# Modulation weights of the retention stage loaded from GpSimd's DMA queue instead of SyncE's

## The chip, the cores and the metric

The kernel runs on one core of a Trainium2 chip. The metric is the device time of one execution in microseconds (us). The engines are named as in the profile: PE is TensorE (matmuls; its weight loads are listed apart as PEld), DVE is VectorE, ACT is ScalarE, POOL is GpSimd and SP is SyncE. SP computes nothing here; it issues DMAs.

## The reference, cut to what matters

One layer of a diffusion backbone for 128 context tokens and 1024 latent tokens with 1024 channels. A modulation vector is computed from a conditioning vector, and its six parts scale, shift and gate the rest of the layer:

```python
mod = jnp.einsum('bd,de->be', jax.nn.silu(cond), w_mod[l]) + b_mod[l]
sh1, sc1, g1, sh2, sc2, g2 = jnp.split(mod[:, None, :], 6, axis=-1)
h = layer_norm(x) * (1.0 + sc1) + sh1
y, sd, sr = mixer(h, ...)
x = layer_norm(ALPHA * x + g1 * y, ln1_w[l], ln1_b[l])
h = layer_norm(x) * (1.0 + sc2) + sh2
f = jnp.einsum('btf,fd->btd', jnp.square(jax.nn.relu(jnp.einsum('btd,df->btf', h, w_ff1[l]) + b_ff1[l])),
               w_ff2[l]) + b_ff2[l]
x = layer_norm(ALPHA * x + g2 * f, ln2_w[l], ln2_b[l])
```

The weight w_mod has 1024 rows and 6144 columns in float32, 24 MB. The mixer has two groups of heads side by side: gated DeltaNet (4 heads, chunked, with a small triangular inverse per chunk) and multi-scale retention (4 heads, chunks of 128 tokens, rotary embedding on the latent tokens only, a normalisation per head). Both read the modulated input h through one projection w_in. An output projection, the gate and a feed-forward part with squared ReLU follow.

## The kernel before, in words

The 1152 tokens are nine tiles of 128. The work goes through stages one after the other: the start (lines 280 to 346: layer norm, the first modulation, h split into a high and a low part so that three fp32r matmuls give nearly fp32), the retention heads (lines 420 to 606), the DeltaNet heads (lines 609 to 1052), the output projection with the second layer norm (from line 1055), and the feed-forward (from line 1138). All DMAs of the kernel are issued by the helper `dma` (lines 85 and 86) from SP's queue.

The modulation vector is made in twelve blocks of 512 columns. `mod_block` (lines 215 to 238) calls `mod_raw_mm` (lines 200 to 213), which loads the weights of a block in pieces of 512 rows by w columns into a tile of 128 partitions by 4 by w, and multiplies each of its four row groups with the two conditioning vectors (`cs`). The sums go to PSUM ("co"), ACT copies them (tile "part", line 219), small matmuls add up the four groups (lines 222 and 231), and DVE adds the bias. The first four blocks are made in the start stage by `mod_early` (lines 312 to 315) with w=512: eight loads of 1 MB each through four buffers. The other eight are made in the retention stage by `r_mod` (lines 478 to 480) with w=256 and two buffers: 32 loads of 512 KB each, rows of 1 KB. Both tiles have the tag "wm". One of these 32 loads has eight matmul records in the trace, called a group here. With two buffers a load can be issued only when the group two before it has been read.

In the retention stage the order of the steps is written by hand in the string `RET` (line 28), which `run` (lines 269 to 277) reads: V projects values, K and Q project keys and queries and rotate them, Z scales the keys, S makes the states, O the outputs, N normalises, T transposes and stores, M makes two modulation blocks, and D is the decay for the DeltaNet stage. A number behind "^" gives a step that much more priority. From this and from what waits for what, a planner sets the order of the instructions in each engine's queue and puts in the waits; every engine then works strictly in that order. An instruction that waits thus holds up all that stand behind it in its queue, and this holds for a DMA's issue too.

What else these queues carry in this stage:

- SP: the weights of the projections ("wr", 256 KB, line 165), rope's copies with swapped halves ("sw", line 439, four of 128 KB each), the copies of the queries ("qd", lines 499 and 500), initial states ("sst"), stores of finished heads ("OT<-oe", line 601) and of states, and the wm loads.
- POOL: rope's product with the sines (line 440), the decay of the query copies (line 501), and the power -1/2 of the normalisation (line 157, called in line 582).
- PE: the projections (line 194, three matmuls for each of eight row blocks), the retention matmuls (lines 490 to 563) and the modulation groups (line 209).

Of the kernel before, what the change touches and what calls it, by code (L numbers as in the profile page):

```python
# [80 lines left out]
def layer_kernel(ctx: ExitStack, tc: tile.TileContext, A, O):  # L81
    nc = tc.nc
    V, S, G, T = nc.vector, nc.scalar, nc.gpsimd, nc.tensor

    def dma(out, in_):
        nc.sync.dma_start(out=out, in_=in_)
# [38 lines left out]
    def pss():  # L125
        turns["s"].append(turns["s"].pop(0))
        return pt(turns["s"][-1])
# [25 lines left out]
    def sb(pool, shape, tag, bufs=1, dt=F32):  # L153
        return pool.tile(shape, dt, tag=tag, name=tag, bufs=bufs)
# [45 lines left out]
    def mod_raw_mm(pool, tag, bufs, e0, n, pp, w):  # L200

        p = pp()
        for c0 in range(0, n, w):
            for i in range(2):
                raw = sb(pool, [128, 4, w], tag, bufs)
                src = w_mod[512 * i:512 * i + 512, e0 + c0:e0 + c0 + w]
                dma(raw, src.rearrange("(k p) c -> p k c", p=128))
                for q in range(4):
                    T.matmul(
                        p[32 * q:32 * q + 32, c0:c0 + w], cs[:, 4 * i + q, :], raw[:, q, :], start=(i == 0), stop=(i == 1),  # L210
                        tile_position=(0, 32 * q),
                    )
        return p

    def mod_block(pool, tag, bufs, e0, n, spool, stag, sbufs, pp=pss, pq=pss, w=512):

        p = mod_raw_mm(pool, tag, bufs, e0, n, pp, w)
        part = sb(spool, [128, n], stag, sbufs)
        S.copy(out=part, in_=p[:, 0:n])
        q = pq()  # L220
        if e0 // 1024 in (2, 5):
            T.matmul(q[0:2, 0:n], sel, part, start=True, stop=True)
            brow = sb(spool, [128, n], stag, sbufs)[0:2]
            dma(brow, A["b_mod"][0:1, e0:e0 + n].to_broadcast([2, n]))
            V.tensor_tensor(out=brow, in0=q[0:2, 0:n], in1=brow, op=ALU.add)
            v = 0 if e0 // 1024 == 2 else 2
            dma(GD[v:v + 2, e0 % 1024:e0 % 1024 + n], brow)
        else:
            m = n // 128
            for j in range(m):  # L230
                T.matmul(q[:, 2 * j:2 * j + 2], part[:, 128 * j:128 * j + 128], sel, start=True, stop=True)
            e = e0 // 128
            V.tensor_tensor(
                out=modT[:, e:e + m, :], in0=q[:, 0:2 * m].rearrange("p (a b) -> p a b", b=2),
                in1=vec1[:, 16 + e:16 + e + m, None].to_broadcast([128, m, 2]), op=ALU.add,
            )
            if e0 // 1024 in (1, 4):
                V.tensor_scalar(out=modT[:, e:e + m, :], in0=modT[:, e:e + m, :], scalar1=1.0, scalar2=None, op0=ALU.add)
# [45 lines left out]
    with tc.tile_pool(name="start", bufs=1) as st:  # L284
# [16 lines left out]
        p = pss()  # L301
        T.transpose(p[:, 0:73], r1, ident[0:73, 0:73])
        V.tensor_copy(out=vec1, in_=p[:, 0:73])
        p = pss()
# [753 lines left out]
    k = 3  # L1058
# [497 lines left out]
```

## Time and profile before

| | |
|---|---|
| Median of three timed runs | 1589.14 us (1587.22 to 1591.74) |
| The profiled execution, whole | 1597.36 us |
| Its span, first to last instruction | 1595.5 us |
| Mean granted TensorE clock | 0.977 |
| Busy DVE / ACT / POOL | 1057.4 / 724.6 / 333.4 us |
| DMA queue used by the program | one, hardware_dynamic: 227249 packets, 246.13 MB, 48.5% of 16 engines |
| wm loads in the retention stage | 32 of 512 KB, issued from 81.0 to 271.8 us |

The times of rows are microseconds from the span's start. A row of the order of time gives start, duration, engine, line, operation, out<-in and a count of merged instructions; in brackets stands how long the engine was idle before it and what ended that. A row of the waits gives the waiting engine and line, what it waited for, the total, the number of times and the longest. SPq and POOLq are the issuing of those engines, which isn't counted as busy time. A row of groups by line gives the busy time, the mean of one in ns, and the idle time before it with what ended most of it. A profile is of one execution, and it can differ from the timed ones.

### The profile page before, as it was taken

The page shows a single profiled execution, that of the slowest core. Times are in us where ns is not written, and L with a number is a line of the kernel's source. Part 1 is how long each engine was busy: PE and PEld are TensorE (multiplying, and loading weights), DVE is VectorE, ACT ScalarE, POOL GpSimd, SP SyncE. Part 2 cuts the span into 40 slices and gives each one's busy share as a digit, 9 for nine tenths or more (in the row PEclk, how much of TensorE's full clock was granted, in tenths as well). Part 3 has the DMA queues.
Part 4 walks back from the last instruction along what each step waited for, and adds up shares of the span by engine and source line. Part 5 has one row for each costly group of instructions (what it writes and reads, how often), then busy time and mean ns, then how long its engine had stood idle before and what let it go on. Part 6 is the DMA issues. An engine that isn't in the chain of part 4 may idle for free.

```text
span 1595.5 us, 26235 instructions
## 1 busy us (share of the span) xinstructions
PE 1507.1 (94%) x9597; PEld 1328.6 (83%) x9597; DVE 1057.4 (66%) x2045; ACT 724.6 (45%) x1562; POOL 333.4 (21%) x328
## 2 busy tenths in 40 slices
PE   4899999899999999999798999999999999999997
PEld 2697676898898989987687999999998788888885
DVE  4415424568795788657894576656666887867887
ACT  4522312564564464352457565445554453443411
POOL 2201021211112022100541035556553000000000
PEclk9799999999999999999898999999999999999998
DMA  9233556332323123454345944443347989878511
GB/s 347 74 82 83 172 157 200 77 78 70 82 49 102 37 58 108 122 163 161 104 152 158 292 154 139 154 155 128 125 139 260 333 281 315 290 237 284 169 54 66
DMA packets 227378, 247.81 MB, mean 155 GB/s; under 512 B 35956, under 2 KB 161889, under 8 KB 227121
## 3 DMA queue, kind: packets, MB, share of 16 engines
q1 hardware_dynamic: 227249, 246.13, 48.5%
q8 instruction: 76, 1.25, 0.3%
q14 instruction: 53, 0.43, 0.1%
HBM read 185.72 MB, written 56.15 MB: 152 GB/s over the span
## 4 chain that ended last, share of the span: by engine, by line
PE 51%; DVE 10%; issue 4%; ACT 3%; DMA 2%; POOL 2%; SPq 0%; DVEq 0%; POOLq 0%; ACTq 0%
PE d L1252 18%; PE m L1416 14%; PE mm L194 7%; PE d L194 3%; PE p L1416 2%; DVE lnst L245 2%; PE c L900 1%; PE c L891 1%; PE c L884 1%; DVE qk L638 1%; PE co L915 1%; PE co L914 1%; DVE wl L161 1%; DVE acc L1491 1%; POOL lnmv L157 1%
## 5 line engine op out<-in xcount | busy, mean ns | idle before, releaser
L194 PE MATMUL mm<-hH,wh 128*128 128x384 f32 x696 | 247.4, 356 | 2.0 <-ACT raw L634 2.0
L194 PE MATMUL mm<-hL,wh 128*128 128x384 f32 x696 | 246.6, 354 | 0.0
L194 PE MATMUL mm<-hH,wl 128*128 128x384 f32 x696 | 245.7, 354 | 0.0
L161 DVE TENSOR_TENSOR wl<-wr,wh 128x512 fp32r<-128x512 f32 (+1 forms) x149 | 126.8, 855 | 118.3 <-ACT wh L160 109.4
L1416 PE MATMUL m<-vh,sh 128*128 128x512 f32 x460 | 180.6, 393 | 3.4 <-DVE af L1308 3.0
L1416 PE MATMUL m<-vl,sh 128*128 128x512 f32 x460 | 179.8, 393 | 1.4 <-DVE vl L161 1.3
L1416 PE MATMUL m<-vh,sl 128*128 128x512 f32 x460 | 179.6, 391 | 0.4 <-DVE sl L161 0.4
L194 PEld LDWEIGHTS mm<-hH,wh 128*128 128x128 f32 x696 | 133.9, 192 | 7.3 <-ACT raw L634 2.2
L194 PEld LDWEIGHTS mm<-hL,wh 128*128 128x128 f32 x696 | 133.5, 192 | 5.5 <-issue 4.1
L194 PEld LDWEIGHTS mm<-hH,wl 128*128 128x128 f32 x696 | 133.4, 192 | 4.9 <-issue 3.7
L160 ACT CAST wh<-wr 128x512 fp32r<-128x512 f32 (+1 forms) x149 | 88.9, 613 | 78.8 <-PE mm L194 52.2
L1252 PE MATMUL d<-sh,wl 128*128 128x288 f32 x416 | 122.9, 295 | 0.5 <-DVE wl L161 0.5
L1252 PE MATMUL d<-sh,wh 128*128 128x288 f32 x416 | 122.7, 295 | 0.6 <-ACT wh L160 0.6
L1252 PE MATMUL d<-sl,wh 128*128 128x288 f32 x416 | 122.6, 295 | 0.0
L160 ACT CAST sh<-ar 128x512 fp32r<-128x512 f32 x103 | 63.8, 619 | 94.1 <-PE m L1416 46.1
L1416 PEld LDWEIGHTS m<-vh,sh 128*128 128x128 f32 x460 | 86.7, 189 | 22.9 <-issue 3.8
L157 POOL TENSOR_TENSOR lnmv<-lnmv,ex 128x1 f32<-128x1 f32 x36 | 22.0, 612 | 396.4 <-DVE lnmv L249 379.4
L1416 PEld LDWEIGHTS m<-vl,sh 128*128 128x128 f32 x460 | 86.5, 188 | 20.9 <-DVE vl L161 2.1
L1416 PEld LDWEIGHTS m<-vh,sl 128*128 128x128 f32 x460 | 86.8, 189 | 19.1 <-DVE sl L161 0.8
L161 DVE TENSOR_TENSOR sl<-ar,sh 128x512 fp32r<-128x512 f32 x103 | 70.7, 688 | 33.6 <-ACT sh L160 27.6
L1252 PE MATMUL d<-hH,wh 128*128 128x288 f32 x312 | 91.5, 294 | 0.0
L160 ACT CAST vh<-br 128x512 fp32r<-128x512 f32 x103 | 63.8, 619 | 48.9 <-DVE br L1380 32.2
(394 smaller groups left out, 3677.1 us busy)
## 6 DMA issues: line engine op xcount, KB each, us to landing
br<-in_w_ff_dram SPq DMA_DIRECT2D x168, 256.0 KB
ar<-HS SPq DMA_DIRECT2D x91, 256.0 KB
HS<-hL SPq DMA_DIRECT2D x65, 256.0 KB
wm<-in_w_mod_dram SPq DMA_DIRECT2D x32, 512.0 KB
wr<-in_w_in_dram SPq DMA_DIRECT2D x56, 256.0 KB
af<-HX SPq DMA_DIRECT2D x20, 576.0 KB
wm<-in_w_mod_dram SPq DMA_DIRECT2D x8, 1024.0 KB
w3h<-in_w_ff_dram SPq DMA_DIRECT2D x13, 512.0 KB
```

Of the source, the lines that this page charges most:

```text
L157: G.tensor_tensor(out=out, in0=in_, in1=ex[:, 0, 0:n], op=ALU.pow)
L160: S.copy(out=pool_hi, in_=src)
L161: V.tensor_tensor(out=pool_lo, in0=src, in1=pool_hi.bitcast(F32), op=ALU.subtract)
L194: T.matmul(p[:, 0:384], x[:, k % 4, :], y[c][:, k, :], start=(k == 0 and a == 0), stop=(k == 7 and a == 2),)
L245: V.bn_stats(out=st[:, j, :], in_=x[:, 512 * j:512 * j + 512])
L638: V.scalar_tensor_tensor(out=y, in0=raw[:, tap:tap + 1156], scalar=vec2[:, 12 * tap + ct:12 * tap + ct + 1], in1=y, op0=ALU.mult, op1=ALU.add,
L884: T.matmul(p[:, 0:128], qk[:, 0, off(n):off(n) + 128], old, start=True, stop=True)
L891: T.matmul(p[:, 0:128], UP[:, m_, 0, :], r, start=True, stop=True)
L900: T.matmul(p[:, 0:128], kt[:, n, :], y2, start=True, stop=True)
L914: T.matmul(p[:, 128:256], qk[:, 1, off(n):off(n) + 128], old, start=True, stop=True)
L1252: T.matmul(p[:, q, :], w[x][:, k, :], hs[y][:, k, CH * q:CH * q + CH], start=(k == 0 and a == 0), stop=(k == 3 and a == 2),)
L1416: T.matmul(p, x[i], w[j], start=(first and a == 0), stop=(last and a == 2))
```

## The change

In `mod_raw_mm` the load of the weights is issued by GpSimd where w is under 512, by SyncE otherwise. The calls with w=256 are those of the retention stage; those of the start stage have w=512. Tiles, sizes, buffers, matmuls and the strings of the order are the same.

```diff
@@ -204,7 +204,7 @@
             for i in range(2):
                 raw = sb(pool, [128, 4, w], tag, bufs)
                 src = w_mod[512 * i:512 * i + 512, e0 + c0:e0 + c0 + w]
-                dma(raw, src.rearrange("(k p) c -> p k c", p=128))
+                (nc.gpsimd if w < 512 else nc.sync).dma_start(out=raw, in_=src.rearrange("(k p) c -> p k c", p=128))
                 for q in range(4):
                     T.matmul(
                         p[32 * q:32 * q + 32, c0:c0 + w], cs[:, 4 * i + q, :], raw[:, q, :], start=(i == 0), stop=(i == 1),
```

## The prediction

> **What bounds the kernel now.** I read the page first, then the stretches of the retention stage, then who waited for whom there, and then the order of time of three engines around the loads that move.
>
> ```profile
> span 1595.5 us, 26235 instructions
> ...
> PE 1507.1 (94%) x9597; PEld 1328.6 (83%) x9597; DVE 1057.4 (66%) x2045; ACT 724.6 (45%) x1562; POOL 333.4 (21%) x328
> ```
>
> The profiled execution has a span of 1595.5 us and took 1597.4 us as a whole; the median of the three timed runs is 1589.1 us, 8.2 us less. The sums below are made on the profiled execution's own rows, and what they change is then put onto the median. A measurement of this kernel can tell about 0.3%, 4.8 us, from no change. TensorE (PE) is the engine to look at, and the next view shows how full it is where the moved loads lie.
>
> ```profile
> 80.00:160.00 80.00, 79.92 (x541) 70.05 (x542) 27.32 (x61) 17.53 (x38) 11.68 (x5) 1.00 0.33 82
> 160.00:222.00 62.00, 56.14 (x389) 44.02 (x383) 21.15 (x68) 16.93 (x33) 4.96 (x3) 0.94 0.54 163
> 222.00:290.00 68.00, 67.07 (x454) 50.17 (x455) 33.70 (x85) 15.31 (x31) 10.01 (x4) 1.00 0.58 169
> 208.00:214.50 6.50, 6.50 (x25) 6.40 (x25) 2.79 (x4) 0.92 (x2) 2.36 (x1) 0.50 0.09 32
> ```
>
> The columns are the stretch, its length, busy time of PE, of its weight loads, of DVE, ACT and POOL, then the granted clock, the DMA share and GB/s. Between 80 and 290 us PE is idle for 0.08, 5.86 and 0.93 us, 6.87 us in all. The fourth row is a stretch in which PE was busy at half its clock: 6.5 us that hold some 3.25 us of work. So all that any better feeding of this stage can give back is about 10 us, 0.6%. POOL works 4.96 of 62 us and 10.01 of 68 us: as an engine it has room.
>
> ```profile
> L86 SPq DMA_DIRECT2D wm<-in_w_mod_dram x32: 367/374/732, 81.0 to 271.8; - x32
> PE co L209 <- DMA wm<-in_w_mod_dram: 5.7, 4, 3.6
> SPq L86 <- PE co L209: 36.3, 19, 5.6
> L160 ACT CAST wh<-wr 128x512 fp32r<-128x512 f32 x17 | 10.4, 619 | 26.1 <-PE mm L194 25.9 <-DMA wr<-in_w_in_dram 0.2
> ```
>
> The first row counts what moves: 32 loads of tile wm, whose issue holds SP for 0.374 us (median). The second says that nearly all of PE's idle time there, 5.7 of 6.87 us, is waiting for just these loads, four times, 3.6 us at the longest. The third is the cost on SP's side: 36.3 us in which SP stood still until PE had read a wm buffer, with the other transfers queued behind. The fourth asks who suffered from that: the projection weights (wr), the traffic that feeds most of PE's work, made ScalarE wait for 0.2 us. The stops of SP's queue are thus long, but they end no wait of PE. What ends one is the time from a free wm buffer to its landed data.
>
> **The change, part by part.** 32 issues leave SP and go to POOL. The 8 early loads with w=512 stay on SP. Bytes, tiles, buffers (two) and matmuls are the same.
>
> *What SP saves.* 32 x 0.374 = 12.0 us of issue time and the 36.3 us of waits. I put this at nothing, because of the 0.2 us above. The cover is the work that PE still has from weights loaded earlier; were it gone, SP's lateness with wr would cost time in the kernel before, which the change would give back, and those 0.2 us are its bound. The queued transfers that go earlier are rope's copies (sw), the state queries (qd) and stores (OT).
>
> *What POOL takes on.* The 32 issues, the waits for a free buffer, and behind them in POOL's queue the rope products (L440), the query products (L501) and the small powers (L157). How long a load takes from POOL's queue isn't in this trace, since POOL issues no DMA in it. So the extra time e from free buffer to landed data is bounded by rows of POOL's own instructions, of which SP's 0.37 us of issue is taken off.
>
> ```profile
> L157 POOL TENSOR_TENSOR lnmv<-lnmv,ex 128x1 f32<-128x1 f32 x36 | 22.0, 612 | 396.4 <-DVE lnmv L249 379.4 <-DVE lnmv L247 16.9
> L157 POOL TENSOR_TENSOR ms<-ms,ex 128x9 f32<-128x9 f32 x3 | 5.4, 1804 | 72.6 <-DVE ms L581 72.6
> L440 POOL TENSOR_TENSOR sw<-sw,cosin 128x1024 f32<-128x1024 f32 x4 | 11.7, 2918 | 79.6 <-DMA sw<-kT 57.0 <-DMA sw<-qT 22.6
> ```
>
> The shortest arithmetic of the stage's kind takes 0.612 us, the longest 2.918 us, so e lies between 0.24 and 2.55 us. A gain of e below nothing isn't excluded by a row (a queue of its own might be served sooner); it is the second rival. I take the row in the middle, 1.804 us for an instruction that touches only 9 elements a partition and so is mostly a program that POOL runs: e = 1.4 us.
>
> *What of it reaches PE.* A load is issued when the group of matmuls two before it has freed its buffer, and it is needed when its own group's turn comes. The room is the distance between the two, and rows of the order of time give it.
>
> ```profile
> 160.68 0.37 SPq L86 DMA_DIRECT2D wm<-in_w_mod_dram  x1
> 197.81 2.03 SPq L86 DMA_DIRECT2D wm<-in_w_mod_dram  x2
> 269.07 0.37 SPq L86 DMA_DIRECT2D wm<-in_w_mod_dram  x1
> ```
>
> ```profile
> 164.82 0.64 PE L209 MATMUL co<-wm,cs 128*32 128x256 f32 x8
> 182.42 0.59 PE L209 MATMUL co<-wm,cs 128*32 128x256 f32 x2 [1.32 <-DMA wm<-in_w_mod_dram]
> 188.35 0.63 PE L209 MATMUL co<-wm,cs 128*32 128x256 f32 x6
> 191.38 0.64 PE L209 MATMUL co<-wm,cs 128*32 128x256 f32 x8
> 193.39 0.64 PE L209 MATMUL co<-wm,cs 128*32 128x256 f32 x8
> 197.11 0.64 PE L209 MATMUL co<-wm,cs 128*32 128x256 f32 x8
> 198.77 0.64 PE L209 MATMUL co<-wm,cs 128*32 128x256 f32 x8
> 201.65 0.64 PE L209 MATMUL co<-wm,cs 128*32 128x256 f32 x8
> 207.15 0.64 PE L209 MATMUL co<-wm,cs 128*32 128x256 f32 x8 [3.59 <-DMA wm<-in_w_mod_dram]
> 238.81 0.64 PE L209 MATMUL co<-wm,cs 128*32 128x256 f32 x8
> 243.96 0.64 PE L209 MATMUL co<-wm,cs 128*32 128x256 f32 x8
> 273.78 0.64 PE L209 MATMUL co<-wm,cs 128*32 128x256 f32 x8 [0.62 <-DMA wm<-in_w_mod_dram]
> ```
>
> The group at 197.11 ends at 197.75, and SP issues at 197.81: a lag of 0.06 us. SP isn't late with these loads, so POOL can't be much earlier. The load issued at 197.81 is used at 201.65 without a wait: it landed within 3.84 us. I take 3.8 us for landing now, 3.8 + 1.4 = 5.2 us after the change; where PE waits already, the whole e is added. A wait also gives the next load, which is under way by then, the same time, so of neighbours only what exceeds the wait before counts.
>
> - Issued 160.68, used 164.82: room 4.14, new wait 5.2 - 4.14 = 1.06.
> - Used 182.42, waited for already: 1.4.
> - Freed by the group at 188.35 (end 188.98, issue 189.04), used 193.39: room 4.35, wait 0.85. The load after it (freed by 191.38, used 197.11) has 5.03 and is covered by that 0.85.
> - Freed by 193.39 (issue 194.09), used 198.77: room 4.68, wait 0.52.
> - Issued 197.81, used 201.65: room 3.84, 1.36 - 0.52 = 0.84.
> - Freed by 198.77 (issue 199.47), used 207.15, waited for already: 1.4 - 0.84 = 0.56.
> - Freed by 238.81 (issue 239.51), used 243.96: room 4.45, wait 0.75.
> - Issued 269.07, used 273.78, waited for already: 1.4.
>
> Sum 1.06 + 1.4 + 0.85 + 0.52 + 0.84 + 0.56 + 0.75 + 1.4 = 7.4 us, all on the path: PE is full on both sides of each wait, and the stage's later work comes behind it in PE's order. On the median: 1589.1 + 7.4 = 1596.5 us. At e = 0.24 the same steps leave 0.24 (182.42), 0.20 + 0.04 (201.65, 207.15) and 0.24 (273.78), 0.7 us: 1589.8. At e = 2.55 (landing 6.35) they give 2.21 + 2.55 + 2.00 + 1.67 + 0.84 + 1.71 + 1.90 + 2.55 = 15.4 us: 1604.5.
>
> The Trainium skill speaks against the move as well, but less: "DMA: Bandwidth & Descriptors", section "Specifications", gives some 1 us to the first byte on the path of a DMA from GpSimd and 0.6 us on that from Sync. By that page e would be 0.4 us and the sum, by the steps above, 0.06 + 0.4 + 0.36 + 0.04 + 0.4 = 1.3 us, 1590.4 as an estimate from it. No run so far shows a DMA from POOL in this kernel, so the page can't be checked yet; it is a further ground for the first rival.
>
> I cost the new order of the instructions at nothing: the planner puts the same work in its own order for the changed queues, PE has other matmuls ready between the groups, and its idle share here is small. It could move some rooms up and others down, and I have no row for either.
>
> **The rivals.** *First, the load costs the same from either queue.* For it: POOL is mostly idle, and SP's issue is only 0.374 us of the 3.8 us to landing, so most of a load is transfer, which doesn't change. Then e stays at its lower end and the time is 1589.8, no difference that can be measured. Against it: rooms of 3.84 and 4.14 us leave next to nothing spare.
>
> *Second, the loads land sooner and the kernel is faster.* What speaks for it is the worst load, seen on SP:
>
> ```profile
> 199.89 2.47 SPq L86 DMA_DIRECT2D sw<-qT  x4
> 202.40 1.12 SPq L86 DMA_DIRECT2D OT<-oe  x2
> 218.11 0.32 SPq L86 DMA_DIRECT2D OT<-oe  x1
> 218.52 0.39 SPq L86 DMA_DIRECT2D wm<-in_w_mod_dram  x1
> 219.00 0.52 SPq L86 DMA_DIRECT2D qd<-qT  x1
> ```
>
> The load issued at 199.47 was needed at 203.56 and landed at 207.15, twice the usual time, while six other transfers of the same queue were issued behind it; and right after that stop of 3.59 us came the 6.5 us at half clock. If a separate queue keeps such loads apart, 3.59 goes, with it 3.25 of lost clock, and the waits of 1.32 and 0.62: 8.8 us, 1580.3. Against it: that load stood ahead of the six, not behind; it shares the DMA engines with them from any queue; and the profiled execution is 8.2 us above the median, so the timed runs may not have that stop at all.
>
> *Third, POOL's queue is held up by a waiting load, and the kernel is slower by another wait.* POOL's instructions behind a load wait for the buffer that PE frees.
>
> ```profile
> 208.31 2.36 POOL L440 TENSOR_TENSOR sw<-sw,cosin 128x1024 f32<-128x1024 f32 x1 [16.50 <-DMA sw<-qT]
> 212.54 1.23 DVE L442 TENSOR_TENSOR qT<-qT,sw 128x1024 f32<-128x1024 f32 x1
> 221.30 0.64 PE L209 MATMUL co<-wm,cs 128*32 128x256 f32 x8
> ```
>
> Take the load whose buffer is freed by the group at 221.30 (end 221.94). If the planned order puts it ahead of the rope product that could begin at 208.31, that product starts 13.6 us late. Rope's last step ended at 213.77 and its result was fetched from 219.00, so 5.2 us of this are spare: 8.4 us late for everything on qT, which PE's order reaches soon after. With the likeliest case's 7.4 that is 15.8 us, 1604.9. It decides as soon as one load is ahead of a rope or query product by more than 5.2 us. For it: the same happened on SP, where a load whose buffer was free at 207.79 stood until 218.52 behind a store (the 218.11 row), so the plan and the chip can differ by 10 us. Against it: POOL has few such products in the stage, and a planner that sees them ready first puts them first. That a load doesn't move is no rival: every one of the stage has w=256.
>
> **How the numbers follow.** The likeliest case, longer landings with POOL's order harmless, gets 0.42; of this 0.30 lies over 4.8 us and 0.12 under it (e below about 1). The first rival gets 0.18, all within 0.3%. The second gets 0.20, of which 0.18 gains over 4.8 us and 0.02 less. The third gets 0.20, all slower. So faster 0.18, same 0.12 + 0.18 + 0.02 = 0.32, slower 0.50. The prediction is 1596.5 us. As cases of both signs hold chance, the range goes from 1584.0, which takes in the smaller gains and leaves out the larger half of the second rival (0.1), to 1610.0, which holds both bounds of e and the third rival's price with 5 us to spare for a second hold-up (0.08 left out). The likeliest case alone runs from 1589.8 to 1604.5.
>
> **What would show it.** Right: POOL rows with 32 DMA issues of wm of more than 0.6 us each; PE's wait for wm in the stage up from 5.7 to 10 us or more, over six times or more, instead of four; SP's waits for co gone; PE's idle time of 6.87 us up by about 7. The first rival shows as waits of 5 to 6.5 us. The second shows as a stage with less than 2 us of waits for wm and no stretch at clock 0.5. The third shows as a rope or query product on POOL that starts right after a load, ACT or DVE waiting for POOL, and PE waiting for qd or sw's results rather than for wm. The prediction is wrong in its ground if the difference arises after 290 us, or if PE's order changed so much that the groups no longer stand 4 to 5 us after the release of their buffers.

## The result and the profile after

| | before | after |
|---|---|---|
| Median of the timed runs, side by side | 1590.44 us (1587.22 to 1592.42) | 1609.18 us (1606.92 to 1610.38) |
| Ratio, 95% interval | | 1.0118 [1.0091, 1.0144] |
| The profiled execution | 1597.36 us | 1608.21 us |

The changed kernel is slower by 18.7 us. The forecast was 1596.5 us, 7.4 us more than before: the direction and the range hold, the size is 2.5 times the forecast. The profiled execution of before is 7 us above its median, so the two traces show only 10.8 of the 18.7 us, and sizes below come from the timed ratios where there are any. Part of that gap lies ahead of the stage: the first matmul of L490 begins at 81.3 us in before and at 77.5 us in after, and from there to the last of L1120 (862.8 and 872.3 us) the kernel after takes 13.3 us more.

The page of the kernel after, and the same three stretches as in the prediction, with one more behind them:

```profile
span 1606.3 us, 26261 instructions
...
PE 1508.3 (94%) x9597; PEld 1330.5 (83%) x9597; DVE 1063.2 (66%) x2045; ACT 724.3 (45%) x1562; POOL 357.5 (22%) x360
...
q0 software_dynamic: 4608, 16.78, 3.3%
```

```profile
80.00:160.00 80.00, 79.92 (x547) 69.68 (x546) 29.98 (x69) 15.78 (x34) 14.72 (x8) 1.00 0.29 70
160.00:222.00 62.00, 54.63 (x397) 42.22 (x395) 19.72 (x59) 17.06 (x34) 18.68 (x19) 1.00 0.66 198
222.00:290.00 68.00, 60.69 (x406) 44.31 (x407) 35.65 (x102) 14.62 (x30) 17.48 (x16) 0.97 0.44 134
290.00:320.00 30.00, 23.43 (x124) 23.11 (x123) 12.53 (x14) 16.39 (x45) 5.49 (x6) 0.89 0.32 84
sum 240.00, PE 218.66 PEld 179.32 DVE 97.88 ACT 63.85 POOL 56.38; mean PE 54.66 PEld 44.83 DVE 24.47 ACT 15.96 POOL 14.09
```

The same four stretches of before end in this row (the last 30 us, which the prediction left out, had 25.57 us of busy PE):

```profile
sum 240.00, PE 228.70 PEld 188.35 DVE 96.05 ACT 67.02 POOL 35.03; mean PE 57.17 PEld 47.09 DVE 24.01 ACT 16.76 POOL 8.76
```

Between 80 and 320 us PE is idle for 240 - 218.66 = 21.3 us, before for 11.3 us: 10 us more. The place is the retention stage and its seam to the DeltaNet heads, the stretch in which the one stage ends and the next begins. Who waited on PE in 60 to 320 us after, two of the same rows before, and who waited on POOL after:

```profile
PE co L209 <- DMA wm<-in_w_mod_dram: 10.9, 11, 2.4
PE s L652 <- ACT qk L642: 6.6, 1, 6.6
PE s L595 <- DVE o L584: 2.7, 1, 2.7
```

```profile
PE s L652 <- ACT qk L642: 3.1, 1, 3.1
PE s L595 <- DVE o L584: 1.3, 1, 1.3
```

```profile
POOL wm L207 <- PE co L209: 71.5, 22, 7.6
```

The waits for wm went from 5.7 us in four to 10.9 us in eleven. The other two rows were 3.1 and 1.3 us before: 4.9 us more, and their names hold no wm load. In the kernel before they lie behind 290 us, where the prediction's stretches ended. What POOL pays for a load:

```profile
L207 POOL DMA_DIRECT2D wm<-in_w_mod_dram x32: 748/748/957, 70.6 to 256.6; - x32
DMA to landing us min/median/max: 3.9/4.7/9.0
```

```profile
190.23 0.64 PE L209 MATMUL co<-wm,cs 128*32 128x256 f32 x8 [1.18 <-DMA wm<-in_w_mod_dram]
```

```profile
191.20 0.75 POOL L207 DMA_DIRECT2D wm<-in_w_mod_dram  x1 [2.32 <-PE co L209]
```

The group ends at 190.87 and POOL issues at 191.20: a lag of 0.33 us, where SP had 0.06. From issue to landing it is 4.7 us (median), where the SP load of the prediction was within 3.84. So e is about 0.33 + 4.7 - 0.06 - 3.84 = 1.1 us, an estimate that sets a median against the bound of one load. The DMA packets of the two traces allow a like comparison of the 32 loads: from SP a load's first packet starts 1.06 us after its issue and its last one ends after 3.67 us (medians), from POOL 1.54 and 4.20 us. By these e is (0.33 - 0.06) + (4.20 - 3.67) = 0.8 us.

### The profile page after: what moved, and what is told of

It reads as the page before. It is cut to its first block, busy times and chain, and to the rows that moved or that the text cites. A ratio compares the mean times of both kernels' runs of the same rounds, so it can differ in the third digit from the quotient of the medians.

```text
span 1606.3 us, 26261 instructions
## 1 busy us (share of the span) xinstructions
PE 1508.3 (94%) x9597; PEld 1330.5 (83%) x9597; DVE 1063.2 (66%) x2045; ACT 724.3 (45%) x1562; POOL 357.5 (22%) x360
## 3 DMA queue, kind: packets, MB, share of 16 engines
q1 hardware_dynamic: 210353, 229.35, 44.7%
q0 software_dynamic: 4608, 16.78, 3.3%
## 4 chain that ended last, share of the span: by engine, by line
PE 55%; DVE 10%; ACT 5%; issue 4%; DMA 4%; POOL 3%; SPq 1%; DVEq 0%; POOLq 0%; ACTq 0%
PE d L1252 16%; PE m L1416 14%; PE mm L194 11%; PE d L194 3%; PE p L1416 2%; DVE lnst L245 1%; PE c L900 1%; DVE qk L638 1%; PE c L891 1%; ACT tmp L1124 1%; PE co L915 1%; PE c L884 1%; SPq L86 1%; PE co L914 1%; DVE tm L730 1%
## 5 line engine op out<-in xcount | busy, mean ns | idle before, releaser
L157 POOL TENSOR_TENSOR lnmv<-lnmv,ex 128x1 f32<-128x1 f32 x36 | 21.7, 604 | 398.7 <-DVE lnmv L249 381.4
```

Source lines behind the costliest of these rows:

```text
L157: G.tensor_tensor(out=out, in0=in_, in1=ex[:, 0, 0:n], op=ALU.pow)
```

## The experiments

The question was where the other 11 us come from. The diff moves 32 DMAs, and the planner, which sees other queues, made another order on every engine. Compared place by place, the two traces differ on all five engines, on PE in 1496 of some 9580 matmuls, from 165 us on to 587 us, well into the DeltaNet heads. So one theory is the landing (a load from POOL lands later and PE waits), the rival is the new order. "Held to an order" below means that every engine's sequence is copied from the other kernel, by order-only dependencies, and only the wm loads are free; in the traces of the first two such runs the sequences are those of the other kernel, but for four neighbouring matmuls in one of them. Each ratio is to the kernel before on the same chip.

**The kernel before again.** No edit.

> The kernel before, unchanged, for a second trace of it. If the profiled execution of before (1597.4 us, 7 us over its timed median of 1590.4) was an odd one, this one takes about 1590 us, and the stop of 3.59 us at 203.56 us with the stretch at half clock behind it is gone from the trace. If those are the kernel's own, they stand there again and the time is about 1597 us.

```profile
PE co L209 <- DMA wm<-in_w_mod_dram: 3.6, 2, 2.3
```

The profiled execution took 1596.02 us. The stop of 3.59 us is one of 2.3 here: it belongs to the kernel, but its size varies.

**Queue and order taken apart.** First the changed kernel in the order of before, then the kernel before in the order of after:

```diff
-    close_fe2()
+    in_order(tc, nc); close_fe2()
...
```

The function `in_order` (left out here) lays down the sequences of the other kernel for all engines, without the wm loads.

> The changed kernel (loads from POOL), with every engine's order of instructions pinned to the order of before; only the 32 loads themselves stand in POOL's queue. Landing theory: what costs is the longer way of each load on POOL's queue (0.33 us to the issue and 0.75 us of issue, against 0.06 and 0.37 before: about 0.9 us); the rooms of the prediction with 0.9 us give 0.56 + 0.9 + 0.35 + 0.02 + 0.84 + 0.06 + 0.25 + 0.9 = 3.9 us, so 1594 us, and if the whole loss is of this kind, 1609. Order theory: what costs is the new order that the planner made for all engines; then this one is within 3 us of before, 1587 to 1594.

> The kernel before (loads from SP), with every engine's order of instructions pinned to the order of the changed kernel; only the 32 loads are in SP's queue instead of POOL's. Landing theory: no loss, 1587 to 1594 us. Order theory: most of the 18.7 us stays, 1602 us or more. If both hold, 1600 us, with the 4 us of the loads missing.

POOL's queue in the old order: 1599.78 us, ratio 1.0052 [1.0022, 1.0082], +7.4 us. SyncE's queue in the new order: 1609.54 us, ratio 1.0126 [1.0092, 1.0161], +17.2 us. The first is above the 1594 us that either theory's sum had at most, the second is what the order theory had. The order costs most of it without any load on POOL, and the two don't add: in the new order the queue makes no difference that can be measured. The waits of the first, then of the second:

```profile
PE co L209 <- DMA wm<-in_w_mod_dram: 7.6, 8, 2.0
PE s L652 <- ACT qk L642: 2.7, 1, 2.7
PE s L466 <- DVE kT L442: 2.5, 1, 2.5
```

```profile
PE co L209 <- DMA wm<-in_w_mod_dram: 8.5, 6, 3.5
PE s L652 <- ACT qk L642: 6.4, 1, 6.4
PE s L466 <- DVE kT L442: 2.8, 1, 2.8
PE s L595 <- DVE o L584: 2.7, 1, 2.7
```

The long waits at L652 and L595 go with the order, not with the queue. A reservation: this order was planned for POOL's queue, and on SP the loads stand among other transfers.

The wait of 2.5 us at L466 in the first is new and is not a load's. It waits for rope's last product on the keys (L442). DVE and POOL of this run, then the same two of the kernel before:

```profile
227.41 3.35 DVE L442 TENSOR_TENSOR kT<-kT,sw 128x1024 f32<-128x1024 f32 x1 [2.29 <-POOL sw L440]
```

```profile
227.34 2.34 POOL L501 TENSOR_TENSOR qd<-qd,xi 128x1024 f32<-128x1024 f32 x1
```

```profile
229.86 1.23 DVE L442 TENSOR_TENSOR kT<-kT,sw 128x1024 f32<-128x1024 f32 x1 [2.29 <-POOL sw L440]
```

```profile
231.67 2.37 POOL L501 TENSOR_TENSOR qd<-qd,xi 128x1024 f32<-128x1024 f32 x1 [1.85 <-DMA qd<-qT]
```

In the kernel before POOL waited 1.85 us for the copy of the queries, and DVE's product ran alone in 1.23 us. With the wm loads off SP's queue that copy lands earlier, POOL starts its product 0.07 us ahead of DVE's, and DVE's takes 3.35 us. These 2.1 us are most of the wait, and SP's freedom costs them, in the kind of place the prediction had put at nothing. The three runs with GpSimd's queue in this order all have the long product (3.35, 3.35 and 3.37 us), the four traces with SyncE's don't (1.23 us each). In one of the four, with half loads, DVE's product started 0.08 us ahead, and there POOL's is long, 3.41 us. The Trainium skill ("SBUF — State Buffer", section "SBUF: two separate sides") has such a rule, that DVE, in an instruction with two inputs in SBUF, and GpSimd share one pair of ports and the one that starts second waits for the whole instruction; the rows agree, since DVE's end (230.76) is POOL's (229.68) and some 1.1 us more.

**More lateness on POOL.** To the first of these two kernels a fill of half the buffer is added ahead of each load:

```diff
-                dma(raw, src.rearrange("(k p) c -> p k c", p=128))
+                _ = w < 512 and MORE.append(int(G.memset(raw[:, 0:2, :], 0.0).ins.name[2:])); (nc.gpsimd if w < 512 else nc.sync).dma_start(out=raw, in_=src.rearrange("(k p) c -> p k c", p=128))
...
```

`MORE` only keeps the fills' numbers, which the held order needs.

> As the run with POOL's queue and the old order, and ahead of each of the 32 loads POOL fills half of its buffer with zeros (overwritten by the load; the result is the same), which makes every load later by some 0.5 to 0.7 us. Landing theory: PE's waits for wm grow with it, by the rooms at 1.5 us in all 1.16 + 1.5 + 0.95 + 0.62 + 0.84 + 0.66 + 0.85 + 1.5 = 8.1 us, so about 4 us more than without the fill. Order theory: no more than 1 us over the run without the fill.

1610.64 us, ratio 1.0137 [1.0104, 1.0171]: 10.9 us over the kernel without the fill, more than twice what the rooms give. The fill takes 0.526 us. In the traces the waits for wm rose only from 7.6 to 11.3 us, but the granted clock fell too (third figure from the end):

```profile
160.00:222.00 62.00, 56.10 (x364) 43.07 (x364) 16.56 (x54) 16.08 (x31) 22.08 (x30) 0.89 0.50 153
222.00:290.00 68.00, 58.57 (x372) 42.42 (x368) 28.33 (x69) 11.69 (x24) 26.37 (x30) 0.92 0.55 160
```

A clock of 0.89 over 62 us and of 0.92 over 68 is at most 12 us of lost work; in the kernel without the fill, at 0.97 in both stretches, it was 4. This trace is the slowest of the kernel's six runs (1621.17 us), so how the 10.9 us divide between waits and clock isn't shown.

**The seam to DeltaNet covered.** My theory was that the new order leaves too little PE work (62 matmuls instead of 99) between the projection of the first DeltaNet head (step P0) and the first transposes, L652. P0 gets a higher priority, in the kernel after and, as control, in the kernel before; a third run goes further with the latter.

```diff
-    DEL = "P0 i0 v0^1000 ..."
+    DEL = "P0^400 i0 v0^1000 ..."
```

> The kernel after, with the priority of step P0 (the first DeltaNet head's projection) raised by 400: the planner puts that projection earlier, and 261 instead of 62 matmuls stand on PE between its last one and the first transpose of DeltaNet (L652). The loads stay on POOL's queue, and the last modulation group stands at about the same place in PE's order (1105 instead of 1100). Theory that the end of the stage is what the new order cost (wait of 6.6 us at L652, 1.4 more at L595, some 3 us of half clock behind it): these go, the wm waits of about 11 us stay, and the time is 8 to 11 us under the kernel after, 1599 to 1601 us, ratio to before 1.005 to 1.007. Rival, that the order costs all along the stage and L652 only shows a lateness that then moves to another place: wait at L652 gone, another of about that size in its stead, time within 3 us of the kernel after, ratio 1.010 or more.

> The kernel before, with the same edit of P0's priority: 266 instead of 99 matmuls cover the chain from the projection to the first transpose, the loads stay on SyncE's queue. Theory of the end of the stage: the wait there was small in the kernel before already (at most 2.7 us), so the gain is 0 to 3 us, ratio 0.998 to 1.000, the same. The difference between this and the run above is then the landing alone, some 7 us as in the run with POOL's queue in the old order. Rival, that any re-planned order of this stage costs, whichever it is: slower by 5 us or more, ratio 1.003 or more.

> The kernel before with P0's priority raised by 1000: 400 matmuls stand between the projection and the first transpose, and the last modulation group comes at place 1305 instead of 1165, so the wm loads have more matmuls between them. Theory that rooms of under 5 us between the release of a wm buffer and its next use are what costs PE its waits: the waits for wm fall under those of the kernel before (3.6 us in its last profile), gain up to 5 us, ratio 0.997 to 1.000. Rival, that the retention steps lose as much by standing later: same or slower, ratio 1.000 to 1.006, with new waits at L466 or L595.

The theory misses in all three; of the rivals only the control's came, that any re-planned order costs 5 us or more. On POOL's queue 1617.76 us, 1.0168 [1.0135, 1.0201], slower than the kernel after by some 8 us; the control 1599.56 us, 1.006 [1.003, 1.0089]; the third 1610.64 us, 1.0125 [1.0088, 1.0162]. The wait of 6.6 us ahead of the first transposes is gone, as expected, and nothing was gained by it. The control shows a possible reason, waits that before lacks:

```profile
PE c L779 <- DVE invA L766: 8.0, 1, 8.0
PE s L859 <- DVE vn L852: 4.1, 1, 4.1
```

The edit costs some 8 us by itself on either queue, and with it the queues still lie 18.2 us apart (1617.76 and 1599.56). A seam without cover is thus not the explanation. In the third the waits for wm fell to 1.5 us and it was slower still: with the steps re-planned, waits for wm alone don't tell the time.

**Short landings: a table of eight.** Each of the 32 loads brings half the rows, in both queues and both orders (all engines held). The matmuls read these rows twice, so these four kernels leave out half of the weights and are there for their time alone:

```diff
-                src = w_mod[512 * i:512 * i + 512, e0 + c0:e0 + c0 + w]
+                src = w_mod[512 * i:512 * i + (256 if w < 512 else 512), e0 + c0:e0 + c0 + w]
-                dma(raw, src.rearrange("(k p) c -> p k c", p=128))
+                dma(raw[:, :(2 if w < 512 else 4), :], src.rearrange("(k p) c -> p k c", p=128))
...
-                        ... raw[:, q, :] ...
+                        ... raw[:, q % (2 if w < 512 else 4), :] ...
```

> The kernel before with all engines held to its own order, and each of the 32 loads of the retention stage brings only 2 of its 4 row groups (256 KB instead of 512); the groups of matmuls read these two twice, so half of these weights are left out. Number and shape of the matmuls are the same. It is the base of a table of four: queue (SyncE, GpSimd) by order (old, new), with landing made short. Both theories: the wm waits of the kernel before (3.6 to 5.7 us) and the half clock behind the longest go, 1582 to 1589 us, ratio 0.994 to 0.998.

> The same half loads, from GpSimd's queue, in the old order. Theory that GpSimd's queue costs only through later landing: with some 1.3 us less of transfer the rooms of 3.8 us and more hold, wm waits under 2 us, time within 3 us of the run with SyncE's queue and half loads. Rival, that GpSimd's queue costs by something else than landing (its own products held up, SyncE's transfers going earlier and crowding): the 7.4 us that whole loads cost in this order stay, at least 5 us over the run with SyncE's queue.

> The same half loads, from GpSimd's queue, in the order of the kernel after. Theory that the new order costs by itself (6.6 us at L652, 2.7 at L595, half clock behind the stop): these stay, 8 to 12 us over the two runs in the old order with half loads, ratio to before 1.000 to 1.005. Rival, that nearly all of the 18.7 us is late landing in one form or another, the groups being closer to their buffers' release in this order: the wm waits of 10.9 us and the half clock go, L652's wait shrinks since the steps ahead of it end sooner, and the time is within 4 us of the two others.

> The same half loads, from SyncE's queue, in the order of the kernel after. Theory of the order: the same as the run with GpSimd's queue and this order within 4 us, 8 to 12 us over the old order. Rival: within 4 us of the old order, since the 17.2 us that this order cost with whole loads came from SyncE's queue standing behind loads that wait (18 waits of 31.3 us in all), which short landings ease.

| Ratio to before | whole loads | half loads |
|---|---|---|
| SyncE, old order | 1 | 0.9970 [0.9941, 0.9999] |
| GpSimd, old order | 1.0052 [1.0022, 1.0082] | 1.0018 [0.9996, 1.0040] |
| SyncE, new order | 1.0126 [1.0092, 1.0161] | 1.0014 [0.9985, 1.0043] |
| GpSimd, new order (after) | 1.0118 [1.0091, 1.0144] | 1.0020 [0.9991, 1.0050] |

Down the columns: GpSimd's queue costs 0.5% in the old order, with whole and with half loads, and nothing in the new one. Across: shorter loads gain 0.3% in the old order but 1.1 and 1.0% in the new one, on either queue. So the new order has two costs. One is there with half loads too: 0.44% on SyncE's queue, 7 us, by the two intervals give or take 6. (On GpSimd's nothing, 0.02%: there the old order has its own 0.5%.) The other, some 0.7%, 11 us, goes when the loads are halved. No run says whether it goes with their earlier landing or with their smaller traffic. Against landing alone speaks the lower left of the table: in the new order SyncE's loads, which land earlier than GpSimd's, gain nothing. Of the four expectations that of the first run came; in the second the rival came, in the third and fourth what happened lies between theory and rival.

PE's idle time between 80 and 320 us, in one trace of each (two of before), goes mostly the same way:

| PE idle, of it waiting for wm (us) | whole loads | half loads |
|---|---|---|
| SyncE, old order | 11.3, 5.7 and 8.5, 3.6 | 5.0, none |
| GpSimd, old order | 15.2, 7.6 | 10.6, 2.5 |
| SyncE, new order | 21.7, 8.5 | 10.4, none |
| GpSimd, new order (after) | 21.3, 10.9 | 12.5, 2.7 |

Where the first cost may come from can be read from the traces: with SyncE's half loads the waits at L652 and L595 are 9.3 us in the new order and 3.8 in the old (8.7 and 5.3 with GpSimd's). DVE of the kernel after at the seam, then its ScalarE and POOL, then ScalarE of SyncE's queue with the new order and half loads, then ScalarE of before:

```profile
292.43 5.80 DVE L638 SCALAR_TENSOR_TENSOR qk<-raw,vec,qk 128x1156 f32<-128x1156 f32 x4 [0.98 <-ACT qk L636]
```

```profile
294.59 0.38 ACT L632 COPY raw<-mm 128x256 f32<-128x256 f32 x1
301.52 3.33 ACT L690 ACTIVATE gr<-gr,ngc 128x128 f32<-128x128 f32 x11 [6.55 <-POOL gr L684]
304.87 1.28 ACT L642 ACT_TABLE_LOAD   x1
306.16 1.17 ACT L642 ACTIVATE qk<-qk 128x1156 f32<-128x1156 f32 x1
```

```profile
299.67 3.58 POOL L684 TENSOR_TENSOR gr<-gr,maskfb 128x768 f32<-128x768 f32 x2 [16.27 <-DMA S<-in_state_delta_dram]
```

```profile
288.34 3.33 ACT L690 ACTIVATE gr<-gr,ngc 128x128 f32<-128x128 f32 x11 [6.54 <-POOL gr L684]
291.69 1.28 ACT L642 ACT_TABLE_LOAD   x1
```

```profile
291.41 1.28 ACT L642 ACT_TABLE_LOAD   x1
292.70 1.17 ACT L642 ACTIVATE qk<-qk 128x1156 f32<-128x1156 f32 x1
...
311.87 1.28 ACT L690 ACT_TABLE_LOAD   x1 [3.08 <-DMA gr<-GR]
315.18 0.40 ACT L690 ACTIVATE gr<-gr,ngc 128x128 f32<-128x128 f32 x1 [2.03 <-POOL gr L684]
315.60 1.28 ACT L642 ACT_TABLE_LOAD   x1
316.89 1.17 ACT L642 ACTIVATE qk<-qk 128x1156 f32<-128x1156 f32 x1
```

In the new order eleven activations of the gates (gr, L690) stand in ScalarE's queue ahead of the first L642, the one that L652 waits for. They wait for POOL's product, which waits for a transfer: ScalarE stands for 6.55 us, and DVE had finished L642's input at 298.23, 6.6 us before L642 began with its table load. In the old order the first L642 comes first, the first activation of L690 22 us later, and the first transposes don't wait. But the old order has the same thing in small: its wait of 3.1 us at L652 is for the second L642 (316.89), which stands behind one activation of L690, with 3.08 and 2.03 us of idle ScalarE. So the new order adds 3.5 us at L652 and 1.4 us at L595. By these rows the stop comes from ScalarE's order and not from a lack of matmuls, as I had it in the three runs above. No run moves these activations alone, and the runs with P0 earlier lost this wait without a gain, so what their place costs is argued and not shown.

For the other cost I looked at PE's groups: some of ten neighbours of the kernel after, and of before the first and the last of the same ten, the 19th to the 28th of the 32:

```profile
219.91 0.64 PE L209 MATMUL co<-wm,cs 128*32 128x256 f32 x8 [1.61 <-DMA wm<-in_w_mod_dram]
223.08 0.64 PE L209 MATMUL co<-wm,cs 128*32 128x256 f32 x8 [1.11 <-DMA wm<-in_w_mod_dram]
...
243.62 0.64 PE L209 MATMUL co<-wm,cs 128*32 128x256 f32 x8 [0.31 <-DMA wm<-in_w_mod_dram]
246.05 0.64 PE L209 MATMUL co<-wm,cs 128*32 128x256 f32 x8
```

```profile
233.13 0.64 PE L209 MATMUL co<-wm,cs 128*32 128x256 f32 x8
...
264.82 0.64 PE L209 MATMUL co<-wm,cs 128*32 128x256 f32 x8
```

The ten begin between 219.91 and 246.05, 26.1 us, and in the old order between 233.13 and 264.82, 31.7 us. From a release to the use two groups on it is thus 2 x 26.1 / 9 - 0.64 = 5.2 us on average, waits included, instead of 6.4; the old order's group at 233.13 even has 11.2 us after the release at 221.94. But a load meets its own room and not the average. Counted one by one over the stage, with PE's waits for wm taken off, eleven rooms are under 5 us in the new order and ten in the old. A landing of 5 us is thus not hidden in either, and why the new order waits longer for wm stays open.

**Whole work with short landings.** Four buffers of half the size on SyncE's queue, old order, the same SBUF:

```diff
-            for i in range(2):
-                raw = sb(pool, [128, 4, w], tag, bufs)
-                src = w_mod[512 * i:512 * i + 512, e0 + c0:e0 + c0 + w]
+            for i, n4 in [(0, 4), (1, 4)] if w == 512 else [(i, 2) for i in range(4)]:
+                raw = sb(pool, [128, n4, w], tag, bufs * 4 // n4)
+                src = w_mod[128 * n4 * i:128 * n4 * (i + 1), e0 + c0:e0 + c0 + w]
...
```

> The kernel before, its order held on all engines but for the loads, from SyncE's queue, complete work: in the retention stage each load of 512 KB through two buffers becomes two loads of 256 KB (two row groups each) through four buffers of half the size, 64 loads in all, the same SBUF and the same matmuls. Theory that the landing of a load against a room of 4 to 5 us is what PE pays for here: a half load lands in about 2.5 to 3 us and its room stays near 4 us, the wm waits fall under 2 us as in the run with half loads, 1583 to 1589 us, ratio 0.995 to 0.999. Rival, that what halving gained was the smaller traffic (8 MB less) or that 32 more issues of 0.37 us and waits on SyncE's queue make other transfers late: ratio 0.999 to 1.004, with waits for wr, kT or qd in place of wm.

Ratio 1.0008 [0.9982, 1.0034]: no difference that can be measured, though the waits for wm are nearly gone:

```profile
PE co L209 <- DMA wm<-in_w_mod_dram: 0.7, 2, 0.4
```

The gain that the theory had, 0.1 to 0.5%, didn't come; the rival's time did, though no wait for wr, kT or qd stands on PE in place of wm. So in the old order taking away the 3.6 to 5.7 us of such waits gave no measurable gain, or the 32 more issues took it back, and part of what the half loads gained may be their smaller traffic. No version tried that does the whole work beats the kernel before.

## Why the prediction was right in direction and wrong in size

- *The step that failed* is "I cost the new order of the instructions at nothing". With the loads on SyncE's queue that order alone costs 17.2 us. The ground given for nothing, other matmuls ready between the groups and little idle time, did not carry over to the new order: PE is idle there for 21.7 us between 80 and 320 us, against 11.3 and 8.5 in the two traces of before. And the rooms were read from an order that the changed kernel no longer has. What in the new order costs the 17.2 us is only in part known: the traces name some 5 us at the seam, longer waits for wm, and behind them the half clock.
- *The range* held with luck. Its upper part was there for the largest e and for the third rival. Neither came, and the new order, which cost most, had no term in it; 1609.18 lies 0.8 us under its end.
- *The likeliest case* holds where its own condition holds. With the old order kept, the queue costs 7.4 us, and 7.4 was the sum. But this agrees partly by chance. e is 0.8 to 1.1 us, not 1.4; at 1.1 the same steps give 0.76 + 1.1 + 0.55 + 0.22 + 0.84 + 0.26 + 0.45 + 1.1 = 5.3 us, at 0.8 they give 3.3. The sum also left out rooms under 5.2 us (the loads used at 246.63 and 268.37, for instance, with 4.39 and 4.74), and the interval of the 7.4 us goes from some 3.5 to 13. In the trace the waits for wm rose from 5.7 us (3.6 in the second profile of before) to 7.6 us, and 2.5 us came at L466, which the sum had not. GpSimd's queue costs 0.5% with half loads as well, 7 us. Against SP's run with half loads, the trace of that run names 2.5 us of waits for wm, where SP's has none, 1.7 us at L466, again with a DVE product of 3.37 us beside POOL's, and 1.3 us more at L652. So landing is a part of it, and the collision of DVE and POOL another, which the sum had not.
- *The first rival*, the load costs the same, is refuted for the landing by the packets, 4.20 us against 3.67, and by the lag of 0.27 us more ahead of the issue. The Trainium skill ("DMA: Bandwidth & Descriptors", section "Specifications") gives 1 us against 0.6 us to the first byte, so e = 0.4; the trace agrees for the first packet, 1.54 us against 1.06, and e is larger by the lag.
- *The second rival*, a gain, didn't come: the stop of 3.59 us went, and eleven shorter ones came in its place.
- *The third rival*, POOL's products held up by a waiting load: POOL does stand for 71.5 us in 22 waits, yet in the kernel after no wait of PE in the stage names a POOL product. In the old order the 2.5 us at L466 have a POOL product in them, but through the collision with DVE's and not through a load ahead of it. The rival's mechanism, an in-order queue that stands on an early instruction, did occur, on another engine: ScalarE behind gr.
- *What was to be seen*: POOL's 32 issues of over 0.6 us, SP's waits for co gone, 10 us or more of waits for wm in over six waits: all there. "PE's idle time up by about 7": between 80 and 290 us it is 14.8 us instead of 6.87, and then 2.1 us more behind 290. Of the signs of a wrong ground, a changed order of PE and a loss after 290 us, the first came and the second for these 2.1 us.
- *Open*: why the new order loses 11 us more than the old one on whole loads, and how that divides into waits and half clock, since single traces differ by as much; and why, with the new order, the queue no longer matters.

## What to carry to other kernels

Where a planner sets the order, a one-line change of a DMA's queue is a change of the whole order: cost it as such, or hold the order and time the queue alone. Look at the in-order queues of all engines around the seam of two stages: here eleven activations stood ahead of the one that PE needed, and PE's wait there grew by 3.5 us. And a small delay can cost more than a sum over rooms says: 0.53 us ahead of each load cost 10.9 us in the old order, where the rooms gave 4.

## What the runs showed of the hardware

A load of 512 KB issued by GpSimd appears in a queue of its own kind, software_dynamic, with 4608 packets for 32 loads, 144 each; from SP the same loads make up some 528 packets each in the other queue (227249 packets before, 210353 after). Its issue keeps POOL for 0.748 us against 0.374 us on SP.

Stops of PE are paid twice where a stretch at half clock follows. Two stretches of the kernel after, behind the stop of 2.35 us for wm that ended at 261.5 and behind the 6.57 us at L652:

```profile
261.70:265.10 3.40, 3.40 (x24) 1.98 (x16) 3.27 (x13) 0.78 (x1) 0.00 (x0) 0.50 0.15 42
306.20:312.90 6.70, 5.52 (x21) 5.52 (x22) 0.77 (x4) 5.73 (x22) 0.66 (x1) 0.50 0.00 0
```

Both stretches are at 0.50. The stop of 2.7 us at L595 in the same trace had no such stretch, so the length of a stop alone doesn't decide. The Trainium skill ("TensorE: Matmul & The Clock Gate", section "HAM oscillation — how this bites in real kernels") speaks of idle gaps of over some 3.4 us; here a stretch at 0.50 followed a stop of 2.35 us.
